# First layer's output projection: two heads at a time in seven block products, with the residual kept in DRAM

## The chip, the cores and the metric

The kernel runs on one core of one Trainium2 chip. The metric is the time of one execution on the device, in microseconds. The engines of a core work side by side and wait for one another through semaphores: TensorE (PE in the profile; its weight loads are PEld), VectorE (DVE), ScalarE (ACT), GpSimd (POOL) and SyncE (SP, which here only issues DMAs). Matmul results land in eight PSUM banks; everything else lives in SBUF or DRAM.

## What is computed

A trunk of two layers runs over two groups (`x_prompt` and `x_sample`), each of 512 tokens by 1024. The first layer is differential attention with 8 heads, the second a retention in both directions. Cut to what matters here:

```python
def diff_attention(h, w_in, ..., w_out, lambda_init):
    proj = h @ w_in                       # 1024 -> 4 * 2048: q, k, v, gate
    ...
    p = softmax(s)                        # two maps for each head
    a = p[:, :, 0] - lam * p[:, :, 1]
    o = a @ v                             # 256 columns for each head
    o = rms_norm(o, subln_g, SUBLN_EPS) * (1.0 - lambda_init)
    o = o.reshape(B, S, D_INNER) * silu(gate)
    return o @ w_out                      # 2048 -> 1024

x = x + diff_attention(rms_norm(x, norm_g[0]), ...)
x = x + bidir_retention(rms_norm(x, norm_g[1]), ...)
y = rms_norm(x, final_norm_g)
```

The change is about `o @ w_out` and the sum with x in the first layer.

## The kernel before

**Numbers in two parts.** Each factor of a matmul is split into a high part (a cast on ScalarE, `hi_of`) and the rest (a subtraction on VectorE, `lo_of`), and a product is three matmuls, hi·hi, hi·lo and lo·hi (`PASSES`). So each factor costs a pass of ScalarE and one of VectorE before TensorE can use it.

**Stages.** `make_b` transposes the normed x of both groups and forms seven left factors from four blocks of it. `projections` then runs through units of 256 columns of `w_in`; each unit takes seven products P1 to P7 of blocks in place of eight (a scheme of the Strassen kind), and its results go to DRAM as `qk_d`, `v_d` and `g_d`. The next stage is the first layer's attention; then `make_b` and `projections` come again for the second layer, and last its attention.

**The first layer's attention, by tile.** A tile is 128 queries of one head and group; there are 64. The loop from line 1186 runs, for tile i: `scores` (two maps, three matmuls of 512 columns each, line 1099, into two `sc` banks), `row_max` (VectorE, line 1107), `exps` (ScalarE, line 1115), `combine` (VectorE, lines 1122 to 1125: reciprocal, factor, difference of the maps), `transp` of tile i-1 (line 1135) with a split, `av` of tile i-2 (twelve matmuls of 256 columns, line 1151), the norm of o (`norm_stats`: a square on ScalarE, line 804, three small POOL operations, lines 806 to 811; `norm_apply`, line 816, scales o on ScalarE), and `turned` of tile i-3: `turn_o` transposes o (line 822) and `gate_o` multiplies it by the gate and splits it into `oT` (lines 828 and on).

**Its output product.** After each tile `owe` puts two `out_step` calls on the list `todo`, one for each half of 512 columns. `fill(1, LAG)`, called twice in each turn of the loop, takes one as long as more than four wait. An `out_step` is six matmuls (line 891: two halves of the head's 256 columns, three passes) into a `pj` bank, and VectorE adds the bank to `xN`, the residual in SBUF (line 896). `out_weights` loads and splits the two halves of the head's 256 rows of `w_out`. With the last head, `out_step` also squares its half (line 899), and `finished` stores x to `x_d` in DRAM and scales it for the second layer.

**The second layer's output product** already works on two heads (a pair p) at a time. With tiles 0 and 1 as upper rows, tiles 2 and 3 as lower rows, the two 128-column parts of a head as columns, seven products do the work of eight. `weight_sums` forms the sums of weight blocks in DRAM, by a copy and an adding DMA issued on POOL (`dma_add`). `gate2` gates a tile and, at a head's fourth tile, forms four sums of blocks and splits them. `out2` is one product of six matmuls. `evac_add` (for the first three pairs) combines the banks and adds the result to `x_d` in DRAM with an accumulating DMA on POOL; `evac_last` (last pair) adds into x in SBUF. `w_split` loads and splits the weights of a product, for the next pair as soon as the last use of the present one is issued.

**What sets the order.** The code gives `plan.op` a list of operations with what they read and write. `Plan.arrange` places them on the engines by due times and estimated costs; TensorE may take an operation up to 24 (`WINDOW`) ahead of the code's order, SP issues a load at most 15 us (`AHEAD`) ahead of its due time by the planner's reckoning, and a `dma_add` is held back 5 more. Each engine then runs its list strictly in order, so an instruction that waits holds up all that stand behind it on its engine.

Of the kernel before, what the change touches and what calls it, by code (L numbers as in the profile page):

```python
# [32 lines left out]
LEFT = 2  # L33
LAG = 4
# [4 lines left out]
B_SLOT = dict(B11=0, B21=4, T1=8, T2=12, B22=16, T3=20, T4=24)  # L39
# [29 lines left out]
class Plan:  # L69
# [9 lines left out]
    def __init__(self):  # L79
        self.rings, self.state, self.ops, self.places, self.holds = {}, {}, [], [], {}  # L80

    def op(self, eng, cost, fn, r=(), w=(), lands=0.0, kb=0, load=False, hold=0.0):
# [50 lines left out]
        if hold:  # L133
            self.holds[n] = hold
        return n

    def arrange(self, starts):
# [16 lines left out]
        for n in range(n_ops - 1, -1, -1):  # L154
# [4 lines left out]
            late[n] = min(at, starts[n]) if "PE" in costs else at  # L159
# [93 lines left out]
def trunk_kernel(  # L253
# [86 lines left out]
    def late(kind, i, shape, dt=F32):  # L340

        name = LATE[kind][i]
        if isinstance(name, int):
            return slot(name, shape, dt)
        return place(name, shape, dt, 512 if name[0] in "cme" else 1024)

    def turns(kind, shape, dt=F32):
# [7 lines left out]
                aT1=[0, 1, 2, "os2"], k1=[4], q1=[5], v1=[6, 7], AB=[8, 9, 10], sg1=[12], F1=[13], wa=[20], wb=[21], S4=[22],  # L355
                w=[11, 14, 15, 16, 17, 18, 19, "ws5", "ws6", 23, 24, 25, 26, 27],
                AS=["ws0", "ws1", "ws2", "ws3", "ws4"], O=["m1", "m2", "m3"], rt=["e0", "e1", "e2"], out=["e3", "e4", "e5", "e6", "e7"], R=["m0", "c3"],
                x=["raw0", "raw1", 20, 21, "raw2", "raw3", "os1", "os2"])
# [28 lines left out]
    BUFS = dict(pj=3, sc=2, o=2, tp=1, x0=1, x1=1, y=1, z=1)  # L387
    BANKS = dict(pj=0, sc=3, o=5, tp=7, x0=0, x1=7, y=1, z=2)
# [42 lines left out]
    def dma(out, in_, r, w, kb, eng=None):  # L431
# [3 lines left out]
                kb=kb, load=any(isinstance(k[0] if isinstance(k, tuple) else k, Buf) for k in w))  # L435
# [47 lines left out]
    def make_b(layer, source):  # L483


        def parts(name, k, hi, lo, r):
            t = slot(B_SLOT[name] + k, [P, 2, S])
# [62 lines left out]
    class Unit:  # L550
        def __init__(self, w, c0, kind, done, view=None):
# [6 lines left out]
            self.early = None  # L558
            self.ops, self.x, self.s = {}, {}, {}
# [57 lines left out]
        def product(self, op):  # L617
# [3 lines left out]
            if opens:  # L621
                self.banks[which] = [bank(dict(x="pj", z="sc", y="o")[which], which) for _ in range(n_banks)]
# [202 lines left out]
    def gate_o(o, sg, oT, t):  # L825
        og = work("og", [P, 2, P], 2)
        tok = slice(t * P, (t + 1) * P)
        dve(256, lambda: nc.vector.tensor_tensor(
            og.t, o[:, 256:512].rearrange("p (e c) -> p e c", e=2), sg[:, :, tok], op=ALU.mult), [(o, 1), sg], [og])
# [29 lines left out]
    def fill(n, lag=0):  # L859
        for _ in range(n):  # L860
            if len(todo) > lag:
                todo.pop(0)()
# [700 lines left out]
```

## Time and profile before

| | |
|---|---|
| timed runs (3) | 1858.39, 1853.10, 1858.77 us; median 1858.39 |
| profiled execution | 1852.53 us |
| its span | 1850.6 us, mean granted TensorE clock 0.997 |
| first layer's attention | from 639.6 (first score) to 1052.6 (start of the last output matmul) |
| output matmuls of 512 columns | 768 in the first layer, 672 in the second |
| DMA | 350.30 MB, mean 189 GB/s |

The span is the time from the profile's first to its last instruction; the execution is 1.9 us longer. In the rows below, a group is written as line, engine, operation, output<-input, and shapes; a number in square brackets is the engine's idle time in front of the instruction, and behind the arrow stands what ended it. Durations of matmuls overlap in the pipeline, so distances between starts say what one costs.

### The profile page before, as it was taken

What the parts mean: (1) busy time and instruction counts of PE and PEld (TensorE: products, weight loads), DVE (VectorE), ACT (ScalarE), POOL (GpSimd) and SP (SyncE); (2) the same over time, 40 slices, a digit from 0 to 9 for tenths busy, and PEclk for the clock granted to TensorE, in tenths of its full rate; (3) what the DMA queues carried; (4) which work ended last, traced back from release to release, by engine and by line L of the source; (5) the groups of instructions that cost most, each with busy time, mean ns of one, the idle gap of its engine ahead of it and who ended that gap; (6) DMA issues with size and microseconds to landing.
All of it is one profiled execution on the core that took longest, in us unless ns stands there. A gap on an engine that the chain in (4) does not pass through costs nothing. (4 is left out here: it accounts for less than half of the span.)

```text
span 1850.6 us, 27959 instructions
## 1 busy us (share of the span) xinstructions
PE 1807.7 (98%) x10241; PEld 1562.4 (84%) x10241; DVE 1463.2 (79%) x2518; ACT 984.2 (53%) x2036; POOL 150.7 (8%) x308
## 2 busy tenths in 40 slices
PE   6999999999999999999999999999999999999998
PEld 5788988988988888888888888988898898888886
DVE  7979688688688588888888897776777768777777
ACT  7644444343343465555555875544444447656663
POOL 2000000000000011111111200000000000111111
PEclk9999999999999999999999999999999999999999
DMA  4335645535545774444453425869785679889883
GB/s 167 120 125 173 181 137 161 179 116 182 160 133 170 267 280 170 182 175 155 151 180 126 160 93 184 233 212 282 208 248 164 192 255 306 241 226 265 233 245 136
DMA packets 172032, 350.30 MB, mean 189 GB/s; under 512 B 13796, under 2 KB 73848, under 8 KB 171896
## 3 DMA queue, kind: packets, MB, share of 16 engines
q1 hardware_dynamic: 160448, 327.48, 52.6%
q0 software_dynamic: 11264, 20.98, 7.0%
q8 instruction: 80, 1.31, 0.3%
q14 instruction: 56, 0.46, 0.1%
q10 hardware_dynamic: 184, 0.08, 0.0%
HBM read 223.17 MB, written 142.08 MB: 197 GB/s over the span
## 5 line engine op out<-in xcount | busy, mean ns | idle before, releaser
L630 PE MATMUL bank<-arena,ws 128*128 128x512 f32 x2160 | 514.4, 392 | 3.7 <-DVE e L498 1.8
L630 PEld LDWEIGHTS bank<-arena,ws 128*128 128x128 f32 x2160 | 404.3, 188 | 91.8 <-ACT ws L438 2.0
L630 PE MATMUL bank<-b,ws 128*128 128x512 f32 x1200 | 294.0, 392 | 3.5 <-DVE e L667 3.5
L630 PEld LDWEIGHTS bank<-b,ws 128*128 128x128 f32 x1200 | 224.7, 188 | 53.0 <-DVE e L667 3.0
L441 DVE TENSOR_TENSOR ws<-st,ws 128x512 fp32r<-128x512 f32 (+1 forms) x192 | 148.8, 779 | 78.7 <-ACT ws L438 53.6
L659 ACT COPY c<-bank 128x512 f32<-128x512 f32 x168 | 98.0, 584 | 207.1 <-PE bank L630 137.6
L637 PE MATMUL bank<-ws,arena 128*128 128x256 f32 x1728 | 204.1, 276 | 0.0
L891 PE MATMUL bank<-ws,arena 128*128 128x512 f32 x768 | 202.3, 400 | 0.3 <-ACT m L423 0.3
L637 PEld LDWEIGHTS bank<-ws,arena 128*128 128x128 f32 x1728 | 201.0, 188 | 1.4
L438 ACT CAST ws<-st 128x512 fp32r<-128x512 f32 (+1 forms) x192 | 132.1, 693 | 107.3 <-PE bank L630 70.0
L441 DVE TENSOR_TENSOR ws<-raw,ws 128x512 fp32r<-128x512 f32 (+1 forms) x156 | 128.2, 826 | 71.6 <-ACT ws L438 58.3
L891 PEld LDWEIGHTS bank<-ws,arena 128*128 128x128 f32 x768 | 139.4, 188 | 27.6 <-ACT m L423 0.6
L438 ACT CAST ws<-raw 128x512 fp32r<-128x512 f32 (+1 forms) x156 | 114.3, 738 | 68.0 <-PE bank L630 46.4
L667 DVE TENSOR_TENSOR e<-bank,c 128x512 f32<-128x512 f32 x168 | 115.9, 690 | 31.6 <-PE bank L630 25.7
L637 PE MATMUL bank<-ws,b 128*128 128x256 f32 x960 | 117.4, 277 | 0.0
L1115 ACT ACTIVATE b<-bank,nm 128x512 f32<-128x512 f32 x128 | 87.9, 687 | 53.5 <-DVE nm L1107 52.9
L637 PEld LDWEIGHTS bank<-ws,b 128*128 128x128 f32 x960 | 113.7, 188 | 0.9
L896 DVE TENSOR_TENSOR b<-bank,b 128x512 f32<-128x512 f32 x128 | 87.8, 686 | 32.0 <-PE bank L891 31.9
L1151 PE MATMUL bank<-arena 128*128 128x256 f32 x768 | 107.1, 290 | 0.0
L1099 PE MATMUL bank<-arena 128*128 128x512 f32 x384 | 100.2, 396 | 4.0 <-ACT b L1115 4.0
L1107 DVE TENSOR_REDUCE nm<-bank 128x1 f32<-128x512 f32 x128 | 87.0, 689 | 16.2 <-PE bank L1099 16.2
L1151 PEld LDWEIGHTS bank<-arena 128*128 128x128 f32 x768 | 96.0, 191 | 0.3
(163 smaller groups left out, 2748.2 us busy)
## 6 DMA issues: line engine op xcount, KB each, us to landing
qk<-os SPq DMA_DIRECT2D x192, 256.0 KB, 4.2
arena<-qk SPq DMA_DIRECT2D x80, 512.0 KB, 4.9
raw<-in_da_w_in_dram SPq DMA_DIRECT2D x64, 512.0 KB, 4.9
v<-os SPq DMA_DIRECT2D x60, 512.0 KB, 4.8
arena<-v SPq DMA_DIRECT2D x48, 512.0 KB, 4.2
raw<-in_ret_w_in_dram SPq DMA_DIRECT2D x48, 512.0 KB, 5.4
g<-e SPq DMA_DIRECT2D x48, 256.0 KB, 4.9
x<-b POOLq DMA_DIRECT2D x48, 256.0 KB, 7.0
```

The costliest lines, as they stand in the source:

```text
L438: act(n, lambda: nc.scalar.copy(dst(), src()), r, w)
L441: dve(n, lambda: nc.vector.tensor_tensor(dst(), src(), hi().bitcast(F32), op=ALU.subtract), r, w)
L630: nc.tensor.matmul(ps.t, a[u][0]()[:, k, :], bt[k][:, v, :], start=(opens and k == 0 and i == 0), stop=(k == 3 and i == 2), skip_group_che ...
L637: nc.tensor.matmul(ps[:, (t % 2) * 256:(t % 2) * 256 + 256], bt[k][:, v, t * P:(t + 1) * P], a[u][0]()[:, k, :], start=(opens and t % 2 == ...
L659: act(S, lambda c=c, ps=ps: nc.scalar.copy(c.t, ps.t), [ps], [c])
L667: dve(S, lambda e=e, ps=ps, c=c: nc.vector.tensor_tensor(e.t, ps.t, c.t, op=ALU.add), [ps, c], [e])
L891: nc.tensor.matmul(ps.t, o[a][:, e, t * P:(t + 1) * P], u[b][:, e, :], start=(n == 0), stop=(n == 5))
L896: dve(S, lambda: nc.vector.tensor_tensor(half, ps.t, half, op=ALU.add), [ps, (x, i)], [(x, i)])
L1099: nc.tensor.matmul(s.t, q[:, a, t * P:(t + 1) * P], k[:, b, :], start=(n == 0), stop=(n == 2))
L1107: dve(S, lambda s=s, m=m: nc.vector.tensor_reduce(m.t, s.t, op=ALU.max, axis=AX.X, negate=True), [s], [m])
L1115: act(840, lambda j=j, s=s, m=m: nc.scalar.activation(p[:, j, :], s.t, AF.Exp, bias=m.t, accum_out=sm[:, j:j + 1]), [s, m], [(p, j), (sm, j)])
L1151: nc.tensor.matmul(o[:, 0:256], aT[:, a, j * P:(j + 1) * P], v[b][:, j, :], start=(n == 0), stop=(n == 11))
```

## The change

The first layer's output product takes the second layer's form:

- The functions of the second layer's output (`w_split`, `gate2`, `out2`, `add_to`, `evac_add`, `half_sum`, `evac_last`, `take_x`, `owe2`) move into one function `outputs(layer, xh, done)`, which is called for both layers. `gate_o`, `new_oT`, `new_xN`, `out_weights`, `out_step`, `owe`, `settle` and `LAG` go.
- Tiles are ordered by blocks (pair, group, head of the pair), so that both heads of a pair follow each other in a group. After the second head's fourth tile, 14 products (two rows of seven) go on `todo`. `fill(1)` takes one at each of its two places in a turn, but for one turn in eight at each place.
- During the first layer's projections, the weight sums of the first layer are formed in DRAM, and x is copied into `x_d`. For the first three pairs the results are added to `x_d` by accumulating DMAs on POOL. For the last pair x is loaded (`take_x`), added to in SBUF, squared, stored, and scaled by halves.
- Three products of the first layer's projections (`LEFT1`) are issued among the first attention tiles, and the weights of the first pair are split behind them.
- Places in SBUF of both layers are dealt anew (`LATE`, `B_SLOT`), and copies for the weight sums get the flag `now`, which makes them due where they stand in the code.

```diff
-LEFT = 2
-LAG = 4
+LEFT, LEFT1 = 2, 3
...
-            late[n] = min(at, starts[n]) if "PE" in costs else at
+            late[n] = min(at, starts[n]) if "PE" in costs else min(at, recent[n]) if n in self.nows else at
...
+                S41=[22], wa1=["raw0"], wb1=["raw1"], AS1=["ws0", "st0", 21, "ws1", "st1"],
+                w1=["ws2", "ws3", "ws4", "ws5", "ws6", "st2", 16, 17, 18, 19, 24, 25, 26, 27],
+                x1=["raw0", "raw1", 20, ("e7", "c3"), 12, 13, 23, 22])
...
-    run(proj)
+    for n in range(NH):
+        step(proj, 20)
+        weight_sums(0, n // 2, n % 2, qk_d[0, 0, n // 2, 0])
+        g, t = n // NT, n % NT
+        dma(lambda g=g, t=t: x_d[g, t][:], lambda g=g, t=t: xs[g][0, t * P:(t + 1) * P, :], [qk_d[0, 0, n // 2, 0]],
+            [x_d[g, t]], 512, now=True)
+    step(proj, 7 * len(first_units) - 6 - 20 * NH - LEFT1)
...
     def turned(i):
-        h, g, t = tiles[i]
+        b, t = tiles[i]
         turn_o(st[i]['o'], st[i]['on'])
-        if t == 0:
-            settle(h - 1, g)
-            oT[h, g] = new_oT(g)
-        gate_o(st[i]['o'], sg[h, g], oT[h, g], t)
-        owe(wo1, h, g, t, oT[h, g], finished)
+        gate1(b, t, st[i]['o'], sg[b])
+        if b % 2 and t == 3:
+            owe1(b // 4, b // 2 % 2)
...
     for i in range(N + 3):
+        if i < LEFT1:
+            step(proj)
+        elif i == LEFT1:
+            run(proj)
+            for op in SEQ:
+                w_split1(0, op)
         at(scores, i, N)
         at(row_max, i, N)
         at(exps, i, N)
         at(combine, i, N)
-        fill(1, LAG)
+        if i % 8 != 3 or i > N - 6:
+            fill(1)
         at(transp, i - 1, N)
-        fill(1, LAG)
+        if i % 8 != 2 or i > N - 6:
+            fill(1)
...
-    proj = projections(second_units, 12)
+    proj = projections(second_units, 20)
```

The order of TensorE at the start of attention, first as it was. L1099 are scores, L630 a projection product, L1135 the transposes, L1151 attention times v:

```order
L1099 MATMUL bank_318<-arena 128x512 x3
L1099 MATMUL bank_331<-arena 128x512 x3
L630 MATMUL bank_394<-b_710,ws_461 128x512 x3
L630 MATMUL bank_394<-b_714,ws_461 128x512 x3
L630 MATMUL bank_394<-b_729,ws_461 128x512 x3
L630 MATMUL bank_394<-b_733,ws_461 128x512 x3
L1099 MATMUL bank_318<-arena 128x512 x3
L1099 MATMUL bank_331<-arena 128x512 x3
L1135 MATMUL bank_276<-ident_241,b_5321 128x128 x4
L1099 MATMUL bank_318<-arena 128x512 x3
L1151 MATMUL bank_312<-arena 128x256 x12
```

The same place now, from the end of the first leftover product behind a score. L1068 are scores, L647 a projection product, L1104 the transposes, L1119 attention times v:

```order
L647 MATMUL bank_405<-b_661,ws_452 128x512 x3
L1068 MATMUL bank_342<-arena 128x512 x3
L1068 MATMUL bank_328<-arena 128x512 x3
L1104 MATMUL bank_284<-ident_249,b_5352 128x128 x4
L647 MATMUL bank_405<-b_723,ws_472 128x512 x3
L647 MATMUL bank_405<-b_727,ws_472 128x512 x3
L647 MATMUL bank_405<-b_742,ws_472 128x512 x3
L647 MATMUL bank_405<-b_746,ws_472 128x512 x3
L1068 MATMUL bank_342<-arena 128x512 x3
L1068 MATMUL bank_328<-arena 128x512 x3
L1104 MATMUL bank_284<-ident_249,b_5395 128x128 x4
L1119 MATMUL bank_321<-arena 128x256 x12
```

One projection product stood behind the first scores; two do now, the second in front of the third tile's scores. The first output product stood behind 12 score banks and stands behind 22.

The order of VectorE among the first output products, as it was. L441 are splits, L828 the gate, L896 the sum with the residual, L1107 row maxima:

```order
L441 TENSOR_TENSOR arena<-bank_276,arena 128x512
L828 TENSOR_TENSOR og_5453<-bank_312,os_212 128x256
L896 TENSOR_TENSOR b_205<-bank_418,b_205 128x512
L441 TENSOR_TENSOR arena<-og_5453,arena 128x2x128
L1107 TENSOR_REDUCE nm_5305<-bank_318 128x1
L1107 TENSOR_REDUCE nm_5324<-bank_331 128x1
L896 TENSOR_TENSOR b_206<-bank_368,b_206 128x512
```

And now, at a head's fourth tile in the first block. L1197 and L1200 are the sums of blocks, L457 splits (the row with 128x1024 is one of the weights), L1076 row maxima, L1091 to L1094 the chain of `combine`:

```order
L1200 TENSOR_TENSOR b_5645<-b_5615 128x256
L1091 RECIPROCAL rc_5360<-sm_5439 128x2
L1076 TENSOR_REDUCE nm_5372<-bank_342 128x1
L457 TENSOR_TENSOR arena<-bank_284,arena 128x512
L1092 TENSOR_SCALAR cc_5459<-sm_5439,rc_5360,neglam_5308 128x1
L1076 TENSOR_REDUCE nm_5391<-bank_328 128x1
L1094 SCALAR_TENSOR_TENSOR b_5636<-b_5636,cc_5459 128x512
L1197 SCALAR_TENSOR_TENSOR b_5645<-b_5645,b_5516 128x256
L1200 TENSOR_TENSOR b_5645<-b_5516,b_5615 128x256
L1197 SCALAR_TENSOR_TENSOR b_5645<-b_5645,b_5516 128x256
L457 TENSOR_TENSOR b_5698<-b_5571,b_5657 128x1024
```

The two sums with the residual of each tile are gone; four sums of blocks and the weight splits have come between the row maxima, which the scores' banks wait for.

The order of POOL in the middle of attention, as it was, three operations of the norm for each tile (L806, L807, L811):

```order
L806 TENSOR_SCALAR css_5390<-css_5390 128x1
L807 TENSOR_TENSOR crs_5403<-css_5390,mhalf_235 128x1
L811 TENSOR_TENSOR crr_5407<-crs_5403,rc_5330 128x1
L806 TENSOR_SCALAR css_5467<-css_5467 128x1
L807 TENSOR_TENSOR crs_5479<-css_5467,mhalf_235 128x1
```

And now, with the writes to `x_d` (L899):

```order
L823 TENSOR_SCALAR css_5455<-css_5455 128x1
L899 DMA x_196<-b_8086 128x512
L824 TENSOR_TENSOR crs_5468<-css_5455,mhalf_243 128x1
L828 TENSOR_TENSOR crr_5476<-crs_5468,rc_5457 128x1
L899 DMA x_198<-b_8111 128x512
L899 DMA x_198<-b_8151 128x512
L823 TENSOR_SCALAR css_5466<-css_5466 128x1
```

Writes of sums now stand between the norm's operations and inside them, mostly one at a time, twelve times two in a row.

476 lines of the change are left out of this document (222 added, 254 removed).

## The prediction

> **What bounds the kernel now.** I read the page first, then the windows that cut the span into stages, then the timelines of TensorE and VectorE inside one attention tile, and last the places where TensorE waits.
>
> ```profile
> span 1850.6 us, 27959 instructions
> PE 1807.7 (98%) x10241; PEld 1562.4 (84%) x10241; DVE 1463.2 (79%) x2518; ACT 984.2 (53%) x2036; POOL 150.7 (8%) x308
> ```
> ```profile
> 60.00:640.00 580.00, 579.00 (x3207) 502.25 (x3206) 459.99 (x709) 256.80 (x429) 0.00 (x0) 1.00 0.51 160
> 639.60:664.10 24.50, 20.06 (x106) 16.55 (x105) 19.70 (x37) 17.01 (x41) 2.11 (x7) 0.93 0.82 316
> 665.00:1040.00 375.00, 375.00 (x2175) 322.89 (x2174) 314.93 (x617) 218.36 (x575) 67.63 (x192) 1.00 0.48 172
> 1040.00:1080.00 40.00, 39.19 (x203) 32.36 (x202) 39.29 (x65) 32.98 (x63) 4.63 (x8) 1.00 0.37 125
> 1080.00:1500.00 420.00, 417.51 (x2410) 365.88 (x2408) 318.73 (x491) 204.58 (x342) 15.97 (x16) 1.00 0.69 207
> 1549.00:1800.00 251.00, 244.87 (x1394) 209.66 (x1392) 188.58 (x384) 165.53 (x400) 41.82 (x48) 0.99 0.89 249
> ```
> Each window row gives its length, then the busy time of PE, PEld, DVE, ACT and POOL, the granted clock, the DMA share and GB/s. The stages are the first layer's projections (60 to 640), its attention with the output product (from 639.6, where the first score stands), the change of layers (1040 to 1080), the second layer's projections and its attention. TensorE is the bound nearly everywhere: 375.00 busy of 375 in the stage that the change rewrites. So time leaves with matmuls, unless the new code makes TensorE wait. VectorE is next, with 314.93 of 375, or 84%.
>
> Durations of matmuls overlap, so I price by distances between starts:
>
> ```profile
> 692.42 1.54 PE L891 MATMUL bank<-ws,arena 128*128 128x512 f32 x6
> 693.80 0.60 PE L1135 MATMUL bank<-ident,b 128*128 128x128 f32 x4
> 694.15 1.64 PE L891 MATMUL bank<-ws,arena 128*128 128x512 f32 x6
> 695.63 0.38 PE L822 MATMUL bank<-ident,on 128*128 128x128 f32 x2
> 695.77 1.66 PE L1151 MATMUL bank<-arena 128*128 128x256 f32 x12
> 697.26 1.55 PE L1099 MATMUL bank<-arena 128*128 128x512 f32 x6
> 698.65 1.54 PE L891 MATMUL bank<-ws,arena 128*128 128x512 f32 x6
> ```
> One tile takes 6.23 us: two output products, the transposes 0.35, the turn of o 0.14, attention times v 1.49, two scores 1.39. An output product of six matmuls is 1.38 to 1.39 between starts where nothing delays it. (The page's group row has 400 ns for one of its matmuls; six would be 2.4 us, which the starts contradict.) Without output products a tile is 3.45 us.
>
> ```profile
> 694.61 0.16 DVE L1122 RECIPROCAL rc<-sm 128x2 f32<-128x2 f32 x1
> 694.80 0.27 DVE L1123 TENSOR_SCALAR cc<-sm,rc,neglam 128x1 f32<-128x1 f32 x1
> 695.11 0.75 DVE L1125 SCALAR_TENSOR_TENSOR b<-b,cc 128x512 f32<-128x512 f32 x1
> 695.77 0.69 DVE L441 TENSOR_TENSOR arena<-bank,arena 128x512 fp32r<-128x512 f32 x1
> 696.38 0.42 DVE L828 TENSOR_TENSOR og<-bank,os 128x256 f32<-128x256 f32 x1
> 696.71 0.68 DVE L896 TENSOR_TENSOR b<-bank,b 128x512 f32<-128x512 f32 x1
> 697.30 0.42 DVE L441 TENSOR_TENSOR arena<-og,arena 128x256 fp32r<-128x256 f32 x1
> 697.64 1.22 DVE L441 TENSOR_TENSOR ws<-raw,ws 128x1024 fp32r<-128x1024 f32 x1
> 698.77 1.28 DVE L1107 TENSOR_REDUCE nm<-bank 128x1 f32<-128x512 f32 x2
> ```
> By the same reading, back to back, VectorE pays 0.60 for 512 columns, 0.34 for 256, 1.13 for a weight split of 1024, 1.16 for the chain of reciprocal, factor and combination, about 0.62 for a row maximum (half of 1.28, rounded down). Counting all VectorE instructions from the first to the last row maximum in the order of before with these prices gives 317.5 us; the window of that stretch holds
>
> ```profile
> 639.60:1022.20 382.60, 378.16 (x2180) 324.72 (x2179) 321.97 (x631) 222.39 (x581) 63.07 (x181) 1.00 0.49 181
> ```
> 321.97, so the prices hold to 1.5%.
>
> **The change, part by part.**
>
> *Products.* Before: 8 heads, 2 groups, 4 tiles, 2 halves, so 128 output products. After: 4 pairs, 2 groups, 2 rows, 7 products, so 112. Each is still six matmuls of 512 columns. 16 x 1.39 = **22.2 us less** on the engine that is busy throughout: this is the whole gain.
>
> *The start of attention.* Here output work comes later: before, the first product followed the first tiles; now it needs both heads of a pair, so eight whole tiles, and stands after 22 score banks.
>
> ```profile
> 649.28 1.50 PE L1099 MATMUL bank<-arena 128*128 128x512 f32 x3 [3.56 <-ACT b L1115]
> 650.59 2.62 PE L1151 MATMUL bank<-arena 128*128 128x256 f32 x12
> ```
> Before, the 24.5 us window holds 12 scores, one projection product (2.75), four transposes, three av and two turns, 17.2 us of work: 7.3 us are lost, 4.4 idle and 2.9 in matmuls that ran slow behind the gap (the av at 650.59 lasted 2.62, that at 695.77 lasted 1.66; mean clock 0.93). The leftover projection products among the tiles, now two behind the first scores where it was one, fill that gap. But then VectorE is late next. I counted what stands before the seventeenth tile's first row maximum and its first score. TensorE: 32 scores, 2 projection products, 15 transposes, 14 av, 13 turns, 9 output products, 68.1 us. VectorE: 32 row maxima, 16 chains, 28 of 512, 35 of 256, 7 splits, 75.0 us. Before it was 80.6 and 74.0. So VectorE becomes the bound of the first sixteen tiles. If it were busy without a break, TensorE would lose 6.9; with 5% of gaps (2% in the window from 1040, 16% in that from 665, and here it leads as in the first) the stretch takes 79, and 10.9 is lost. That is **+3.6** on the 7.3 of before; the ends are -0.4 (VectorE gapless) and +13.9 (84% busy, as from 665).
>
> *The middle, tiles 16 to 61.* TensorE 267.4 us (was 282.7), VectorE 240.5 (was 237.7): 90% where it was 84%. VectorE saves 64 additions of 512 (half of 128, since four products of seven go through ScalarE or stay in a bank) and pays for 12 more splits, 64 sums of 256 and larger splits at each head's fourth tile. That is not a new bound on the mean, but it comes in bursts. The nearest rows disagree: 375 us without a loss at 84% VectorE, and the second layer's attention, already written in this way, 6.1 lost of 251. Of those 6.1, 4.7 stand in two stretches where the pair changes:
>
> ```profile
> 1620.00:1640.00 20.00, 17.26 (x93) 14.41 (x93) 14.88 (x30) 11.89 (x29) 2.62 (x3) 0.91 0.87 256
> 1700.00:1720.00 20.00, 18.08 (x103) 14.83 (x102) 14.88 (x28) 13.48 (x32) 2.90 (x4) 1.00 0.91 265
> ```
> ```profile
> 1631.58 1.04 ACT L438 CAST b<-b 128x1024 fp32r<-128x1024 f32 x1 [5.03 <-DMA b<-wP]
> 1633.05 0.69 PE L822 MATMUL bank<-ident,on 128*128 128x128 f32 x2 [2.58 <-ACT on L816]
> ```
> ScalarE stands in its queue at the cast of a new weight that has not landed, behind it stands the scaling of o, and TensorE waits for that. The first layer gets the same casts, at a lower DMA share (0.48 now). I take **+4**, between 0 and 6.5 (6.1 by 267/251), nearer the kernel's own structure than the unbroken row. ScalarE itself has room: 218 of 375, plus 48 copies of a bank, 12 casts and larger splits, about 54, over some 360.
>
> ```profile
> L1430 ACT COPY b<-bank 128x512 f32<-128x512 f32 x12 | 7.0, 582 | 1.6 <-DMA x<-b 1.6
> q0 software_dynamic: 11264, 20.98, 7.0%
> ```
> DMA: the 48 accumulating writes and 16 accumulating weight sums of the second layer are the 20.98 MB of the second row, 7.0% of the span, about 130 us of all engines. The first layer gets as many; two thirds of them fall into its attention, so its share goes to about 0.7, still below the 0.89 of the second layer.
>
> *The change of layers.* 14 products of the last pair now follow the last tile; the residual is loaded into places that free late, added, squared, stored and scaled. TensorE's work from the last score to the last transpose of x grows from 47.9 to 59.0 us, VectorE's from 63.1 to 69.9 up to its last subtraction there. Cover grows more than the load, but the first raw weights must wait for x's places. 0.8 was lost there; I take **+1**, between -0.8 and +4 (a raw load's 5.4 us, less some cover).
>
> ```profile
> raw<-in_ret_w_in_dram SPq DMA_DIRECT2D x48, 512.0 KB, 5.4
> qk<-os SPq DMA_DIRECT2D x192, 256.0 KB, 4.2
> ```
> *First projections.* 24 copies in DRAM enter SP's queue and 16 sums POOL's. A copy waits for a store of q to land (4.2), and raw loads and stores stand behind it; the four raw buffers and seven ws buffers hide that. The second layer's projections carry the same (420 - 417.5 = 2.5 lost against 1.0 in 580): **+0.5**, between 0 and 2.4. *Second layer.* Only places and the loads' order change: **0**, within 2 either way.
>
> Sum: -22.2 + 3.6 + 4 + 1 + 0.5 = **-13.1**. The profiled execution took 1852.5 (span 1850.6 and 1.9 around it), which gives 1839.4; the median of the three timed runs, 1858.4, lies 5.9 above, so the forecast is **1845 us**.
>
> **The rivals.**
>
> *All is hidden* (0.15). VectorE runs gapless at the start and the loads land in time, as in the 375 us row: -22.2 - 0.4 - 0.8 = -23.4, 1835. Against it: 75.0 against 68.1 at the start.
>
> *VectorE and the weight loads take most of it back* (0.19). VectorE is 90% busy at the start (75.0 / 0.9 = 83.3, so 15.2 lost, +7.9), the middle costs 6.5 and 1.3 more of slow clock (the row from 1620 has 0.91), and the raw loads come late at the change of layers: -22.2 + 7.9 + 7.8 + 4 + 0.5 = -2.0, 1856. [...]
>
> *POOL's queue delays the norms, and it ends slower* (0.09).
>
> ```profile
> 691.89 0.22 POOL L806 TENSOR_SCALAR css<-css 128x1 f32<-128x1 f32 x1 [5.10 <-ACT bank L804]
> 698.12 0.82 POOL L806 TENSOR_SCALAR css<-css 128x1 f32<-128x1 f32 x1 [5.09 <-ACT bank L804]
> 700.17 0.47 ACT L816 ACTIVATE on<-bank,crr 128x256 f32<-128x256 f32 x1
> 701.86 0.38 PE L822 MATMUL bank<-ident,on 128*128 128x128 f32 x2
> 1574.57 0.86 POOL L942 DMA_DIRECT2D x<-b  x1 [4.27 <-ACT b L438]
> ```
> Each tile's norm runs on POOL; o is scaled by 700.64 and turned at 701.86, a slack of 1.2. Now 48 writes of 0.87 stand between the norms: one fits, two in a row (twelve times in the order, and three once) are 0.5 late, and one that waits for its sum holds the norm behind it. From 13.1 / 48 = 0.27 us of delay per write on, the gain is gone; at 0.5 it is 24 us, 1869. Against it: the writes are placed well behind their sums. The row of 0.82 is one in which VectorE's weight split (1.22 from 697.64) ran. [...]
>
> *That the products don't get fewer* is excluded: the order has 1344 output matmuls for 1440.
>
> **How the numbers follow.** Forecast 0.57, the rivals 0.15, 0.19 and 0.09. The range 1833 to 1857 takes in the second and half of the third; the other half and the last are left out. 0.3% is 5.6 us, about what a measurement can tell: faster means below 1852.8. Faster 0.57 + 0.15 + 0.05 = 0.77; within 0.3%: 0.14 of the third and 0.02 of the last, 0.16; slower 0.07.
>
> **What would show it.** 672 output matmuls in the first layer with 1.39 per six; 9 to 12 us lost in its first sixteen tiles with VectorE above 90% there; casts of weights on ScalarE with short waits for DMA; turns that don't wait for POOL; 1 to 2 lost at the change of layers. The forecast is wrong if the start loses 17 or more, if each pair change loses 3, or if POOL's writes stand in front of norms for more than 1.2 us.

## The result and the profile after

The changed kernel takes 1844.37 us (median of 11 runs, 1839.73 to 1851.74), the kernel before 1856.87 beside it (11 runs, 1848.03 to 1863.16). The ratio is 0.9947 with a 95% interval of 0.9925 to 0.9968: faster by about half a per cent. The ratio goes by the means, and by it the change is worth 9.8 us; the medians lie 12.5 apart. The profiled execution took 1843.0 us, 9.5 less than that of before.

The page's first lines for the changed kernel, and the stages by window (length, busy PE, PEld, DVE, ACT and POOL, granted clock, DMA share, GB/s): its first sixteen tiles, tiles 16 to 61, the second layer's projections.

```profile
span 1841.2 us, 28138 instructions
PE 1789.9 (97%) x10145; PEld 1543.3 (84%) x10145; DVE 1461.5 (79%) x2544; ACT 1030.9 (56%) x2122; POOL 230.6 (13%) x372
```
```profile
637.50:714.50 77.00, 72.24 (x429) 60.21 (x428) 71.90 (x149) 61.67 (x152) 22.87 (x43) 1.00 0.77 281
714.50:993.00 278.50, 272.55 (x1592) 234.74 (x1591) 238.21 (x482) 197.81 (x493) 100.45 (x183) 0.99 0.83 238
1062.40:1504.00 441.60, 435.20 (x2512) 380.62 (x2511) 326.14 (x502) 210.71 (x352) 15.83 (x16) 1.00 0.68 203
```
TensorE is busy 17.8 us less than before and the span is only 9.4 shorter, so idle time was added. The DMA share of the middle stage rose from about 0.48 to 0.83, more than the 0.7 that was expected. To compare stages, the loss of a stage is its length, from first start to first start, less its matmuls at the prediction's prices. The same stages for both kernels, and for a second profile of the changed kernel taken later (the 7 us from the first score of tile 62 to the last score are in no row):

| stage | before: us / lost | changed: us / lost | changed, second profile |
|---|---|---|---|
| first sixteen tiles | 88.8 / 8.2 | 77.0 / 8.9 | 77.0 / 8.9 |
| tiles 16 to 61 | 286.4 / 3.8 | 278.5 / 11.1 | 277.5 / 10.1 |
| last score to last transpose of x | 51.2 / 3.3 | 62.5 / 3.4 | 62.7 / 3.6 |
| second layer's projections | 436.3 / 2.2 | 441.6 / 10.2 | 434.8 / 3.5 |
| second layer's attention | 333.0 / 22.6 | 329.7 / 19.2 | 330.3 / 19.9 |

(Undisturbed, eight tiles of before show 0.7 of such loss and of the changed kernel 0.4: that is the error of the prices. So the 3.8 of before is this error alone, and some 2.4 of the changed kernel's 11.1 is.) The matmuls removed are worth 22.2 us by these prices. What was given back stands in two stages, the middle of the first layer's attention (+7.3) and the second layer's projections (+8.0, but only +1.3 in the second profile, whose row there is this):

```profile
1063.10:1497.90 434.80, 432.10 (x2512) 378.12 (x2510) 326.28 (x502) 210.46 (x352) 15.85 (x16) 1.00 0.69 206
```

The middle loses in three places, 96 us apart, one at each change of pair. The windows around them, and then the second of them in the timeline. (Behind the third wait the granted clock was 0.50 from 972.4 to 975.8, for 3.4 us, hence the 0.91 there.)

```profile
760.00:780.00 20.00, 18.23 (x111) 15.67 (x110) 16.93 (x30) 13.50 (x32) 6.30 (x12) 1.00 0.85 258
860.00:880.00 20.00, 17.90 (x108) 15.38 (x107) 16.34 (x32) 13.69 (x33) 7.15 (x13) 1.00 0.87 296
960.00:980.00 20.00, 17.92 (x96) 15.13 (x95) 16.96 (x31) 14.07 (x34) 7.16 (x13) 0.91 0.99 285
```
```profile
871.19 1.05 ACT L454 CAST arena<-b 128x1024 fp32r<-128x1024 f32 x1 [3.46 <-DMA b<-w0P]
872.14 0.44 ACT L821 ACTIVATE bank<-bank,rc 128x256 f32<-128x256 f32 x1
...
872.79 0.78 POOL L823 TENSOR_SCALAR css<-css 128x1 f32<-128x1 f32 x1 [6.99 <-ACT bank L821]
...
874.52 0.47 ACT L833 ACTIVATE on<-bank,crr 128x256 f32<-128x256 f32 x1 [1.82 <-POOL crr L828]
...
875.05 0.44 PE L839 MATMUL bank<-ident,on 128*128 128x128 f32 x2 [2.10 <-ACT on L833]
```
Read from the bottom: TensorE's turn of o waits 2.10 for the scaling of o, that for the norm on POOL, that for the squares on ScalarE, and those stood in ScalarE's queue behind a cast that had waited 3.46 for its weight (b<-w0P) to land. POOL had been idle for 6.99, so it was not the cause. In the middle stage, these are the waits of TensorE, and those of ScalarE for the norm and for such loads (total us, times, longest):

```profile
PE bank L839 <- ACT on L833: 6.0, 3, 2.1
```
```profile
ACT on L833 <- POOL crr L828: 6.3, 7, 1.8
ACT arena L454 <- DMA b<-w0P: 6.3, 2, 3.5
...
ACT arena L454 <- DMA b<-in_da_w_out_dram: 3.2, 1, 3.2
...
ACT b L454 <- DMA b<-w0P: 1.0, 1, 1.0
```

### The profile page after: what moved, and what is told of

Same layout as the page of the kernel before. It is cut to its first block, busy times and chain, and to the rows that moved or that the text cites. A ratio compares the mean times of both kernels' runs of the same rounds, so it can differ in the third digit from the quotient of the medians.

```text
span 1841.2 us, 28138 instructions
## 1 busy us (share of the span) xinstructions
PE 1789.9 (97%) x10145; PEld 1543.3 (84%) x10145; DVE 1461.5 (79%) x2544; ACT 1030.9 (56%) x2122; POOL 230.6 (13%) x372
## 5 line engine op out<-in xcount | busy, mean ns | idle before, releaser
L647 PE MATMUL bank<-arena,ws 128*128 128x512 f32 x2160 | 517.4, 393 | 9.4 <-ACT c L676 4.4
L647 PEld LDWEIGHTS bank<-arena,ws 128*128 128x128 f32 x2160 | 404.9, 188 | 99.3 <-ACT c L676 6.1
L647 PE MATMUL bank<-b,ws 128*128 128x512 f32 x1200 | 294.0, 392 | 2.9 <-DVE e L684 2.9
L647 PEld LDWEIGHTS bank<-b,ws 128*128 128x128 f32 x1200 | 224.5, 188 | 52.7 <-DVE e L684 2.3
L1236 PE MATMUL bank<-b,b 128*128 128x512 f32 x800 | 213.5, 398 | 2.4 <-DVE b L1290 1.3
L654 PEld LDWEIGHTS bank<-ws,arena 128*128 128x128 f32 x1728 | 201.9, 188 | 1.3
L457 DVE TENSOR_TENSOR ws<-st,ws 128x512 fp32r<-128x512 f32 (+1 forms) x192 | 147.7, 772 | 65.9 <-ACT ws L454 48.3
L1236 PEld LDWEIGHTS bank<-b,b 128*128 128x128 f32 x800 | 145.5, 188 | 34.5 <-DVE b L1290 2.9
L457 DVE TENSOR_TENSOR ws<-raw,ws 128x512 fp32r<-128x512 f32 (+1 forms) x140 | 107.7, 775 | 54.7 <-ACT ws L454 48.6
L457 DVE TENSOR_TENSOR b<-b,b 128x512 fp32r<-128x512 f32 (+2 forms) x200 | 134.3, 681 | 17.7 <-ACT b L454 17.0
L454 ACT CAST b<-b 128x512 fp32r<-128x512 f32 (+2 forms) x200 | 121.1, 624 | 46.7 <-DVE b L1413 16.3
L899 POOL DMA_DIRECT2D x<-b x96 | 86.6, 947 | 361.9 <-DVE b L1261 232.4
L454 ACT CAST ws<-raw 128x512 fp32r<-128x512 f32 (+1 forms) x140 | 97.2, 701 | 52.4 <-PE bank L647 38.6
L1119 PE MATMUL bank<-arena 128*128 128x256 f32 x768 | 104.6, 286 | 1.0 <-DVE b L1179 0.5
L1068 PE MATMUL bank<-arena 128*128 128x512 f32 x384 | 102.4, 401 | 1.5 <-ACT b L1084 1.5
```

The source lines that it names most:

```text
L454: act(n, lambda: nc.scalar.copy(dst(), src()), r, w)
L457: dve(n, lambda: nc.vector.tensor_tensor(dst(), src(), hi().bitcast(F32), op=ALU.subtract), r, w)
L647: nc.tensor.matmul(ps.t, a[u][0]()[:, k, :], bt[k][:, v, :], start=(opens and k == 0 and i == 0), stop=(k == 3 and i == 2), skip_group_che ...
L654: nc.tensor.matmul(ps[:, (t % 2) * 256:(t % 2) * 256 + 256], bt[k][:, v, t * P:(t + 1) * P], a[u][0]()[:, k, :], start=(opens and t % 2 == ...
L899: plan.op("POOL", 1.0, lambda: nc.gpsimd.dma_start(out(), in_(), accum_op=ALU.add), r, w, lands=5.5, kb=kb, hold=hold)
L1068: nc.tensor.matmul(s.t, q[:, u, t * P:(t + 1) * P], k[:, v, :], start=(n == 0), stop=(n == 2))
```

## The experiments

All are edits of the changed kernel, except the last. Losses are those of the table above; "middle" is tiles 16 to 61. The ratio is to the kernel before, with its interval. Each loss is read from one profile. In the middle stage, the kernels of the rows "changed", "changed, again", "copies not marked" and "no left-over products" have the same instructions in the same order, so their 10.1 to 13.2 is what one program gives there. In the second projections the two profiles of the changed kernel alone give 10.2 and 3.5.

| kernel | first 16 tiles: us / lost | middle lost | 2nd projections lost | ratio |
|---|---|---|---|---|
| changed | 77.0 / 8.9 | 11.1 | 10.2 | 0.9947 (0.9925 to 0.9968) |
| three places for loads | 78.4 / 10.3 | 8.2 | 4.4 | 0.9926 (0.9897 to 0.9955) |
| copies not marked | 76.9 / 8.8 | 13.2 | 6.0 | 0.9947 (0.9927 to 0.9967) |
| no left-over products | 76.1 / 10.7 | 10.3 | 7.2 | 0.9959 (0.9937 to 0.9982) |
| no accumulating writes | 79.2 / 11.1 | 5.7 | 6.0 | 0.9921 (0.9891 to 0.9950) |
| no low parts, first pair | 75.5 / 7.4 | 10.6 | 4.1 | 0.9939 (0.9918 to 0.9959) |
| writes in halves | 76.8 / 8.7 | 14.7 | 4.6 | 0.9944 (0.9925 to 0.9963) |
| later casts | 77.3 / 9.2 | 5.7 | 7.2 | 0.9896 (0.9877 to 0.9915) |
| three places, later casts | 77.6 / 9.5 | 5.2 | 12.8 | 0.9901 (0.9884 to 0.9917) |
| changed, again | 77.0 / 8.9 | 10.1 | 3.5 | 0.9936 (0.9912 to 0.9959) |
| later casts, not marked | 76.7 / 8.6 | 5.3 | 5.5 | 0.9872 (0.9849 to 0.9894) |
| all transfers later | 79.6 / 11.5 | 5.8 | -1.0 | 0.9881 (0.9860 to 0.9902) |
| before, later casts | 85.5 / 4.8 | 3.8 | 6.0 | 0.9963 (0.9943 to 0.9982) |

### Three places for the loads of the weights

```diff
-S41=[22], wa1=["raw0"], wb1=["raw1"],
+S41=[22], wa1=["raw0"], wb1=["raw1"], wc1=[20],
-t = late(("wa", "wb")[cnt_of.setdefault("raw", 0) % 2] + L, 0, [P, 2, S])
+t = late(("wa", "wb", "wc")[cnt_of.setdefault("raw" + L, 0) % (2 if layer else 3)] + L, 0, [P, 2, S])
```


> The first layer's output weights are loaded into three places in turn instead of two, nothing else is changed. Theory A (the 11.1 us lost in tiles 16 to 61 come from ScalarE standing at a cast of a weight that has not landed, 6.3 + 3.2 us of such waits, with the scaling of o queued behind it): the third place lets each load start one product earlier, these waits shrink below 3 us, tiles 16 to 61 lose 6 or less, and the kernel is 4 to 6 us faster than the changed kernel. Theory B (the loss is the burst of casts, splits and accumulating writes itself): the casts no longer wait for the DMA but tiles 16 to 61 still lose 9 or more, and the time stays within 2 us. Theory C (the load of the DMA engines is the limit, 0.85 to 0.99 in those windows): the waits stay above 7 us, time unchanged.

Theory A, in the main. ScalarE no longer waits for any weight in the middle, and of TensorE's waits of 2 at the three pair changes 0.4 is left at two and nothing at the third. The middle still loses 8.2, since two places of its own are in it: 2.1 at a turn of o in the seventeenth tile and 1.25 in front of an output product. The first is a norm that was held in POOL's queue: its square was done at 717.15, an accumulating write stood in front of it and started only at 719.13 (for what, the profile does not show), and the norm began at 719.70. The stage gained 2.9 us where 5 were expected; 0.9926 against 0.9947 does not tell it apart by time alone.

### The copies of the second layer not marked as early

```diff
-dma(..., [key], [t], 512, now=True)
+dma(..., [key], [t], 512, now=layer == 0)
```


> The copies in DRAM of the second layer's weight sums are again placed in SP's queue by the planner's late times, as before the change; the first layer's stay early. Theory A (the 10.2 us lost between the last transpose of x and the first score of the second layer, where 2.2 were lost before, come from these copies, which now stand in pairs ahead of stores of q and k so that ScalarE waits for a place of os): the stretch loses 2 to 5 again, and the kernel is 5 to 8 us faster than the changed kernel. Theory B (the new order of places in the second layer's projections, twelve moved slots and the prefetch of slot 20 instead of 12, does it): the stretch still loses 8 or more and the time stays within 2 us. Nothing ahead of the second layer's projections should move.

Theory A falls short. The stalls moved, from the products at 1151, 1237, 1250 and 1352 us to others (1266, 1363, 1482, near where before had two of its own, 1270 and 1484), but 6.0 are still lost, which lies between the two profiles of the changed kernel (10.2 and 3.5), and the time is the same. One thing did move ahead of the edit: the first projections lost 5.9 instead of nothing, by a cause that has nothing to do with it (its matmuls of 256 columns started every 117.8 ns instead of 113.6, last section).

### No left-over products

```diff
-LEFT, LEFT1 = 2, 3
+LEFT, LEFT1 = 2, 0
```


> No product of the first layer's projections is left over for the first attention tiles (three before); all are done ahead of the first score. Theory A (the leftover products fill time in which TensorE would wait for the first tile's chain and then for VectorE, which has 75.0 us of work before the seventeenth tile): sixteen tiles take 74 to 77 us as now but hold 5.5 us less of TensorE's work, so 13 to 16 are lost there instead of 8.9, and a gap of more than 2.5 us with slow matmuls behind it comes back near the first scores; the kernel is 4 to 8 us slower than the changed kernel. Theory B (VectorE's order alone sets the stretch and it had nothing to do with the products): the stretch gets shorter by 5.5 and the time stays within 2 us.

Between the two. The planner itself still put one projection product behind the first score, so only 2.75 us of work left the stretch, and it got 0.9 shorter: 1.8 more are lost, as A has it per product (2.7 would be all). No gap of 2.5 us came back; the longest wait in the stretch was below 1. A left-over product is worth some 2 us by the stage, and the whole edit not the 4 to 8 of A; the time does not tell it from nothing (0.9959 and 0.9947, with intervals that overlap).

### No accumulating writes in the first three pairs

```diff
-dma_add(lambda: x_d[g, t][...], src, r, [(x_d[g, t], i)], 256)
+if layer:
+    dma_add(lambda: x_d[g, t][...], src, r, [(x_d[g, t], i)], 256)
```


> The 48 accumulating writes of the first layer's first three pairs are left out, so the output lacks their three pairs' products in the residual; the products and their evacuations stay. The forecast's theory (the writes cost nothing: norms have 1.2 us of slack and the DMA has room): tiles 16 to 61 lose 9 to 11 as with them, time within 3 us of the changed kernel. Rival theory (48 writes of 0.95 us in POOL's queue hold norms, and their traffic delays the loads of the weights): at 0.1 to 0.27 us per write 5 to 13 us go, tiles 16 to 61 lose 5 or less, and the waits of the weight casts for their DMA fall from 9.5 us to below 4. The residual read at the end may come earlier; the change of layers should not move by more than 2.

The middle loses 5.7 instead of 11.1, so the writes do cost, about 5 us, and the forecast's theory that they cost nothing falls. (By time it is 4.8 us, with intervals that overlap.) How they cost is read from the loads: the issue rows of this kernel, then of the changed one, for the weight sums (w0P) and the plain weights, and last of the kernel before for its plain weights, with the size and the median us from issue to landing:

```profile
b<-w0P SPq DMA_DIRECT2D x12, 512.0 KB, 3.9
b<-in_da_w_out_dram SPq DMA_DIRECT2D x9, 512.0 KB, 7.2
```
```profile
b<-w0P SPq DMA_DIRECT2D x12, 512.0 KB, 6.3
b<-in_da_w_out_dram SPq DMA_DIRECT2D x9, 512.0 KB, 9.1
```
```profile
raw<-in_da_w_out_dram SPq DMA_DIRECT2D x14, 512.0 KB, 8.8
```
Without the writes a weight sum lands 2.4 us earlier and a plain weight 1.9, the DMA share is 0.54 instead of 0.83, and ScalarE's waits for weights fall from 10.5 us in four pieces (up to 3.5) to 6.8 in five, none above 1.9. A late landing alone cost nothing in the kernel before: its plain weights took 8.8, and in its middle ScalarE never waited for one. The change of layers was not to move by more than 2, and got 2.9 longer.

### The writes in halves

```diff
-dma_add(lambda: x_d[g, t][:, i * S:(i + 1) * S], src, r, [(x_d[g, t], i)], 256)
+for c in (slice(0, 256), slice(256, S)):
+    dma_add(lambda c=c: x_d[g, t][:, i * S + c.start:i * S + c.stop], lambda c=c: src()[:, c], r, ..., 128)
```


> Each of the first layer's 48 accumulating writes is issued as two of 256 columns, so POOL issues 96, with the same bytes moved. The rival of the prediction (POOL's queue holds the norms; 48 more issues of 0.9 us): scalings of o wait for POOL, tiles 16 to 61 lose 20 or more instead of 11.1, and the kernel is at least 10 us slower than the changed one. The forecast's theory (issues on POOL have slack, only their traffic counts, by way of late weights): tiles 16 to 61 lose 9 to 15, the kernel is 0 to 5 us slower.

This parts the queue from the traffic: POOL is busy 145.18 of 282.1 us in the middle where it was 100.45, with the same bytes. Its window, and the wait of the scaling of o for POOL:

```profile
713.80:995.90 282.10, 274.25 (x1593) 234.85 (x1592) 239.70 (x485) 198.04 (x493) 145.18 (x230) 0.99 0.88 236
```
```profile
ACT on L833 <- POOL crr L828: 5.7, 9, 1.3
```
The scalings wait for POOL no longer in total than before (6.3), and the middle loses 14.7, within the 9 to 15 of the forecast's theory and not the 20 of the rival. 3.8 of these stand at the third pair change, where ScalarE waited 4.8 for a weight; the granted clock of the stage was 0.99 (first row above). What the 48 more issues themselves cost TensorE is two waits, 0.5 and 0.3, for norms with writes in front of or between their operations. So POOL's queue is not the cause of the changed kernel's loss; the rival of the prediction falls.

### Low parts of the first pair's weights left out

```diff
+if layer or p:
     lo_of(1024, lambda: lo.t, lambda: t.t, lambda: hi.t, [t, hi], [lo])
```


> The first layer's first pair of heads uses the high parts of its output weights in place of the low parts too, so seven splits of 1024 columns leave VectorE (7 x 1.13 = 7.9 us of the 75.0 counted before the seventeenth tile) and TensorE has the same matmuls; the output lacks these low parts. Theory A (VectorE, 93% busy, sets the length of the first sixteen tiles): the stretch falls from 77.0 to between 70 and 73 and 2 to 5 us are lost there instead of 8.9; the kernel is 4 to 7 us faster than the changed kernel. Theory B (the stretch is held by the first tiles' chain and by waits for loads, VectorE is merely busy): it stays at 75 to 78.

Theory B. In the changed kernel VectorE runs nearly without a break from about the eighth tile on. Still, without the seven splits (7.9 us by the prediction's price) the stretch is only 1.5 shorter; since other work of VectorE moved into it, VectorE's busy time there fell by 5.1, from 71.90 to 66.76:

```profile
667.30:690.00 22.70, 21.04 (x131) 17.65 (x130) 22.66 (x49) 20.26 (x51) 7.51 (x15) 1.00 0.72 262
690.00:714.50 24.50, 23.75 (x142) 19.90 (x140) 24.39 (x53) 19.29 (x48) 10.96 (x16) 1.00 0.70 234
```
```profile
639.10:714.60 75.50, 71.43 (x430) 60.36 (x429) 66.76 (x144) 61.25 (x152) 18.47 (x43) 1.00 0.82 288
```
The first eight tiles lose 4.5 with this edit and 5.3 without it: there is no output product yet to fill TensorE while a tile goes through ScalarE and VectorE. That this chain is what holds them was read from the waits (each below 1.3 us, for exponentials, splits and combinations in turn) and not tried.

### Later casts, and both

```diff
 def dma(..., now=False, extra=0.0):
-    ... lands=2.0 + kb / 200.0,
+    ... lands=2.0 + extra + kb / 200.0,
-dma(lambda: t.t, lambda: src, [src], [t], 512)     # the load of an output weight
+dma(lambda: t.t, lambda: src, [src], [t], 512, extra=4.0)
```


> The planner is told that the loads of the output weights of both layers land 4 us later than it believes now (8.6 instead of 4.6 us), so it puts their casts later into ScalarE's order; buffers and loads stay. Theory A (the pair changes lose because a cast stands too early in ScalarE's queue, ahead of scalings of o): ScalarE's waits for those loads, 9.5 us in tiles 16 to 61, fall below 4 and that stretch loses 6 to 8. Theory B (a cast that is placed later holds its load buffer longer, so the next load starts later, and two buffers are the limit): waits for the loads stay at 6 or more, the loss at 9 or more.

> Both: three places for the loads of the first layer's output weights, and loads that the planner takes to land 4 us later in both layers. If both causes add up, tiles 16 to 61 lose 4 to 6 us, no wait of a weight cast for its load is left in the first layer, and the kernel is 5 to 9 us faster than the changed one. If three places alone had already taken the whole (8.2 lost there, 2.1 of it at one product that has nothing to do with a pair change), the loss stays at 6 to 8 and the time is that of three places, within 2 us.

Theory A of the first. With the same two places and the same bytes, only the order changed, no wait for a weight is left among ScalarE's, and TensorE's own in the middle, with the row of that stage, are

```profile
PE bank L839 <- ACT on L833: 0.3, 2, 0.2
PE bank L1236 <- DVE b L1261: 0.3, 1, 0.3
PE bank L1104 <- DVE arena L457: 0.2, 1, 0.2
```
```profile
714.10:985.80 271.70, 270.68 (x1587) 232.36 (x1585) 235.87 (x477) 195.87 (x492) 106.42 (x183) 1.00 0.84 241
```
The DMA share is still 0.84. The edit moves both ends, casts to later places in ScalarE's queue and some loads to earlier ones in SP's: in this stage of the changed kernel a cast starts as little as 4.1 us behind the issue of its load, with the edit never less than 8.2. So the loss was not a limit of the DMA and not the burst of casts on ScalarE: it was a cast put too close behind its load in an in-order queue, by a planner that took 4.6 us for a load that takes 6.3 to 9. 1834.23 us, 0.9896, is better than the changed kernel by 9.5 us by its first ratio and by 7.4 by its second ("changed, again"). The edit touches both layers: 5.4 of the gain stand in the middle and 2.6 in the second layer's attention. With the third place added the middle loses 5.2 and the time is the same (0.9901): the first theory of that run has the loss right, but hardly any of it comes from the third place, which adds 0.5 us to what the later casts win.

### The changed kernel again, and the second layer's projections

> The changed kernel once more, nothing edited, for a second profile of it. What belongs to the order of the program must stand at the same places: three losses of about 2 us in tiles 16 to 61 where the pair changes, 8 to 11 us lost in the first sixteen tiles, and losses of 0.4 to 1.5 us at the same four products of the second layer's projections. What was chance moves or goes: the windows at half clock, and with the one at 1252 us about 4 of the 10.2 us lost in the second layer's projections, so that 4 to 7 are left there.

The three pair changes lose 1.9, 1.3 and 2.2, the first sixteen tiles 8.9, three of the four products of the second projections 0.4 to 1.2 (the one at 1352 nothing): those belong to the program. With 3.5 lost the second projections came out below the 4 to 7 expected. The rest of the 10.2 was chance: most of one wait of 2.8 that ended at 1252.7, with a granted clock of 0.50 from 1252.3 to 1255.7, and slower matmuls of 256 columns (114.8 ns from start to start instead of 113.6, last section).

> The later-placed casts (loads of the output weights taken to land 4 us later), and in addition the copies of the second layer's weight sums without the early mark. Theory A (the mark costs 3 to 5 us in the second layer's projections): that stretch loses 2 to 4, where 7.2 were lost with the later casts alone, and the kernel is 2 to 5 us faster than with them alone (1834.2). Theory B (the copies' place moves the stalls but doesn't remove them, as 4.9 us in gaps at other products suggested): 5 to 7 are lost, the time within 2 us.

Theory B by the stage (5.5 lost, at other products). The median, 1831.02, is the lowest of all, 3.2 under the later casts alone, but the intervals (0.9849 to 0.9894, 0.9877 to 0.9915) overlap. Either is faster than both kernels of the question.

> The later-placed casts, and the planner takes every other transfer on SP's queue to land 2 us later as well (stores of q and k land after 4.9 to 6.4 us in the second layer's projections, it believes 3.3). Theory A (the stalls left at the four products of the second layer's projections come from casts that wait for places of os whose stores land later than planned): they go, that stretch loses 2 to 4 instead of 7.2, and the kernel is 3 to 5 us faster than with the later casts alone. Theory B (the places of os are simply too few, whatever the order): the stretch loses 6 or more; the time is the same or, since all loads of the first projections move as well, up to 5 us slower.

Theory A for that stage. In the changed kernel its longest stall began with a cast that waits for the store of q before it (first line); with all transfers planned later, TensorE has no break in 430 us (second):

```profile
1250.12 0.62 ACT L454 CAST os<-e 128x512 fp32r<-128x512 f32 x1 [3.04 <-DMA qk<-os]
```
```profile
1072.00:1502.30 430.30, 430.30 (x2511) 378.36 (x2510) 324.04 (x498) 210.37 (x352) 15.84 (x16) 1.00 0.71 209
```
The gain was lost elsewhere: between the last score and the last transpose of x 10.7 are lost, where the later casts alone lose 3.7, since two waits of 3.3 and 1.4 for the operands came up and the granted clock was 0.93 over the 49 us from 1023 (0.85 over the 20 us from 1055), and 5.9 in the first projections by slow matmuls (117.8 ns from start to start, last section). In time it is no better than the later casts alone.

### The kernel before with later casts

The edit is the same for its output weights in both layers.

> The kernel before the change with the same edit of the planner's landing time for its output weights in both layers (4 us later). Theory A (what the later casts win is what the change had lost at its pair changes in the first layer; there the old kernel lost nothing): the first layer's attention is as in the kernel before, 8 and 4 us lost, only the second layer's pair changes get shorter, 2 to 4 us, so 0.998 to 0.999 of the time before. Theory B (the later casts help any order): 5 us or more faster than before.

By time it is theory B: 0.9963, 7 us by the ratio. By stages most of A stands: the middle stayed at 3.8 and the second layer's attention got 2.7 shorter. What A left out is the start, where 4.8 are lost instead of 8.2 (in the kernel before, 2.9 of it in slow matmuls at a granted clock of 0.93 over the first 24.5 us), and the second projections, where 6.0 are lost instead of 2.2. With the planner mended in both kernels the ratio of the two is 0.9896 / 0.9963 = 0.9933, so the change is worth 12.5 us then where it was 9.8; by the intervals that is not a sure difference.

## Why the prediction was right, and where it was not

**The total** was forecast at 1845 and measured at 1844.4. That it is so close is luck in part. The forecast for the profiled execution was 1839.4, and that took 1843.0; the 5.9 us added for the median of three runs was too much, since 11 runs of before gave 1856.9, only 4.3 above the profiled one. And errors of the terms cancelled in part: against its term in the sum the start cost 2.9 less, the middle 3.3 more and the second layer 4.6 more.

**Products, -22.2:** right. 672 output matmuls stand in the first layer's rows, and six of them still cost 1.39 from start to start, so 22.2 left.

**Start, +3.6:** over-estimated; it is +0.7. The loss of 8.9 is just under the 9 to 12 named, with VectorE at 93% (71.90 of 77.00), so the count of 75.0 was right to 4%. (The first output product stands behind 20 score banks in the trace, not behind 22.) The step that failed is the cause put on it, that VectorE is "the bound of the first sixteen tiles": without seven splits, 7.9 us, the stretch was 1.5 shorter. It runs gapless only from the eighth tile on, with ScalarE close behind (20.26 of 22.70), and the rest was lost before. Also part of the 8.2 of before hung on its order: with later casts it was 4.8.

**Middle, +4 between 0 and 6.5:** the mechanism was right in each link (cast waits for its load, scaling of o behind it, turn behind that) and so was the place, the pair changes. The size was off: +7.3 and +6.3 in two profiles, +6.3 to +9.4 over all four of these instructions, from just under the upper end to past it, and some 1.5 more if the error of the prices is taken off both kernels. The wrong step was to scale the second layer's 6.1 us down on account of "a lower DMA share (0.48 now)": with the accumulating writes the share became 0.83 (the prediction's own lines on DMA had 0.7), and the waits at each of three pair changes came out at 2, as high as the second layer's. Without the writes, at 0.54, the stage lost only 1.9 more than before.

**Change of layers, +1:** +0.1 and +0.3. Cover grew as the load did. **First projections, +0.5:** 0.0 in the first profile; in the second 2.1, by matmuls of 512 columns that all ran slower (230.0 ns on the mean instead of 228.9, last section).

**Second layer, 0:** wrong as a single number, in both directions. Its attention got 3 us shorter in both profiles; the first pair change, with a wait of 2.58 and a granted clock of 0.50 from 1632.5 to 1635.8 in before, has neither now:

```profile
1620.00:1640.00 20.00, 19.97 (x113) 16.78 (x112) 13.97 (x29) 12.86 (x32) 2.62 (x3) 1.00 0.93 278
```
Its projections lost 8.0 more in one profile and 1.3 in the other. That stalls move when places and orders change was not priced at all, and it is larger than the 2 allowed for.

**The rivals.** *POOL's queue*: falls as an account of this loss, by the halves. The prediction's slack argument held: 48 more issues cost TensorE two waits of 0.5 and 0.3. That a write can hold a norm is true all the same: with three places for loads one did, for 2.1. And the writes are not free, as the forecast had them: about 5 us by way of later weights. *VectorE and the weight loads take most back*: half of it came, the middle's 7.8 almost to the number, not the start's 7.9. *All is hidden*: no; but with the later casts the kernel comes out at 1834, what that rival gave, since then the middle does hide.

## What to carry to other kernels

When this work was moved onto ScalarE's in-order queue, what counted was where the waiting instruction stood in it, not how busy the DMA was: the middle lost 11.1 at a DMA share of 0.83 and 5.7 at 0.84, and at the second pair change a cast that waited 3.46 for its load held the squares behind it and, by way of the norm, TensorE for 2.10. Compare the landing times that a planner assumes with those of the trace, stage by stage, after each change that adds traffic; here one number, 4.6 for a true 6.3 to 9, was worth nearly as much as the change itself. It cost only where the cast stood close behind its load: the kernel before had the same number and loads of 8.8, and lost nothing by them in its middle. And take two profiles before a loss of a few us in one stage is explained.

## What was not expected of the hardware

*Matmuls of 256 columns ran at two rates.* In two of the fourteen profiles all of the first layer's 1344 such projection matmuls started every 117.8 ns instead of 113.6, 5.7 us in all, though in one of them the instructions of every engine up to there are those of the changed kernel, in the same order. The 512-column ones beside them did not change (229). The same window of the changed kernel and of the one with unmarked copies, x223 and x214 matmuls in 25 us without a break:

```profile
190.00:215.00 25.00, 25.00 (x223) 25.00 (x222) 16.66 (x26) 9.56 (x16) 2.86 (x3) 1.00 0.90 218
```
```profile
190.00:215.00 25.00, 25.00 (x214) 25.00 (x214) 15.84 (x25) 9.44 (x15) 2.86 (x3) 1.00 0.89 228
```
Milder forms (means of 114.8 to 115.7) stand in the second layer of five profiles. In the second profile of the changed kernel it was the other way round: 113.6 for the 256-column ones of the first layer, and 230.0 on the mean for the 512-column ones instead of 228.9, 2.1 us in all. The cause stays open.

*Behind a gap of 2 us the clock fell in one profile and not in the other.* At the third pair change TensorE waited 2.08 us in the first profile of the changed kernel and 1.98 in the second; behind the first, twelve matmuls of 256 columns took 2.04 and six of 512 took 2.76, behind the second 1.67 and 1.56:

```profile
971.34 2.04 PE L1119 MATMUL bank<-arena 128*128 128x256 f32 x12
973.18 2.76 PE L1068 MATMUL bank<-arena 128*128 128x512 f32 x6
```
```profile
971.72 1.67 PE L1119 MATMUL bank<-arena 128*128 128x256 f32 x12
973.22 1.56 PE L1068 MATMUL bank<-arena 128*128 128x512 f32 x6
```
The granted clock was 0.79 over the 8 us from 968 in the first profile, with 0.50 from 972.4 to 975.8, and 1.00 over the 10 us from 966 in the second. Nor did the length of the gap decide in the first profile: behind 2.10 at its second pair change the clock stayed at 1.00 (over the 20 us from 860), behind 2.08 at the third it fell to 0.50. What decides is not shown.
